# A float32r/bf16 QKV projection: another order of the products in a pair, and a padded identity tile

## The chip, the cores and the metric

The kernel runs on one core of a Trainium2 chip. The metric is device time in microseconds of one execution; the time given is the median of several runs, and one further execution was profiled.

In the profile, PE is the matrix engine, PEld its loading of the stationary operand (128 x 128, ahead of each matmul), DVE the vector engine, ACT the scalar engine, POOL the GpSimd engine. SP is used here only to issue DMAs. A matmul here has a stationary operand of 128 x 128 and a moving operand of 128 x 512 or 128 x 256; it adds its result into a PSUM bank of 128 x 512 float32. SBUF is the memory that the operands lie in; an address in the text is a byte offset within each of its 128 partitions.

## The reference

```python
def reference(x, w_qkv):            # x: 16 x 512 x 768, w_qkv: 768 x 2304, float32
    qkv = np.matmul(x, w_qkv)
    q = qkv[..., :768]
    k = qkv[..., 768:1536]
    v = qkv[..., 1536:]
    return np.stack([q, k, v], axis=0).astype(np.float32)
```

So it is one matrix product, 8192 x 768 by 768 x 2304, whose columns are split over three outputs.

## The kernel before

The 8192 rows are cut into 32 blocks of 256 rows, p = 0 to 31. The 2304 columns are cut into two groups of 1024 (q = 0 and q = 1) and 256 columns between them, the direct columns.

For p = 3 to 31 each group of 1024 columns is computed with seven products of half size in place of eight (the Winograd form of Strassen's scheme): the block of x is split into a 2 x 2 of 128 rows by 384, the weights into a 2 x 2 of 384 by 512. One block of rows with one group of columns is a `Quad`, and one pair is the two quads of one block p: a with q = 0 and b with q = 1. `do(u, n)` makes product n of quad u. Every product is three matmuls, one for each 128 of the 384 (L206):

- Products 1 and 2 are bf16: stationary xb (x rounded to bf16, by POOL, L169), moving b1.
- Products 3 to 7 are float32r: stationary s (five sums of blocks of x, made by POOL, L177 to L181), moving t1 to t4 (four sums of weight blocks) or b22 (product 3).

Below, "a6" is `do(a, 6)`, and so on. Every quad uses three PSUM banks. Bank x takes product 1, is copied by ACT into c11 (L220), then takes product 6 on top and is copied into c12 (L227), then 7 into c22 (L233), then 4 into c21 (L237): each of these products waits until ACT has read what was in the bank before. Bank z takes product 2, which DVE adds to c11 (L224). Bank y takes product 5, which DVE adds to c22 (L234), and then 3 on top, which DVE adds to c12 (L240). There are eight banks in all, given out in turn.

`rem(p)` computes the direct columns of a block in bf16: 12 matmuls of 256 columns (L256) into one bank, one copy by ACT (L266), one store by SP (L267). `store_quad` has SP store a quad (L247, L248 for a; L251, L252 for b).

A pair is written out by hand in `two` (p = 3 to 30). Its argument `early` is called behind product 1 of both quads: it has DVE transpose the next block of x (L124), POOL round it and make its sums, and SP and ACT issue the loads of the block after that (L120, two each). Before the change the order is: a1 b1, early, a2 b2, direct columns, a6 b6 a5 a7 b5 b7 a4 a3, store a, b4 b3, store b. The last block (p = 31) runs in `last`, in another order: a1 b1 a2 a6 b2 b6, a5 a7 b5 b7, a4, half of the direct columns, b4 a3 b3, the other half.

Blocks p = 0 to 2 are computed plainly in bf16 (`block`, L381) while the weights arrive and are turned into sums.

The tiles lie in SBUF in the order in which their pools are made. In the program of before the first pool has w_rem at 16512, b1 at 19584 and 25728, b22 at 31872 and 38016, t_0 (the four t of q = 0) at 44160, zero, tiny, and last eye (the identity that PE's transposes use) at 69792, 256 bytes. Behind it come the other pools: t_1 (the four t of q = 1) at 70048 and 82336, bt, o, the staging tiles, orem, xin, xf, xb from 201120 on, and s at 213408 and 221088. Every tile behind eye is a multiple of 512 bytes long. Within b1, b22, the t, xb and s the slices that one matmul takes are 1024, 2048, 2048, 256 and 512 bytes long.

Of the kernel before, what the change touches and what calls it, by code (L numbers as in the profile page):

```python
# [10 lines left out]
def kernel(  # L11
# [20 lines left out]
    nc = tc.nc  # L32
    P = 128
# [15 lines left out]
    bf16 = mybir.dt.bfloat16  # L49
# [9 lines left out]
    w_pool = ctx.enter_context(tc.tile_pool(name="w", bufs=1))  # L59
# [77 lines left out]
    def copy_halves(dst, src, two):  # L137

        nc.vector.tensor_copy(out=dst[0], in_=src[0])  # L139
        if two:  # L140
            nc.scalar.activation(dst[1], src[1], ident)  # L141
        else:
            nc.vector.tensor_copy(out=dst[1], in_=src[1])
# [3 lines left out]
    def cast_rows(p, two=True):  # L147
        src = xin.pop(p)
        xc[p] = s_pool.tile([P, 2, K], bf16, name="xc", tag="s")
        for r in range(2):  # L150
            halves = (slice(0, K // 2), slice(K // 2, K))
            copy_halves([xc[p][:, r, n] for n in halves], [src[:, r, n] for n in halves], two)

    def turn_rows(p, two=True):
        c = xc.pop(p)
        xb[p] = xb_pool.tile([P, KT, 2 * P], bf16, name="xb")
        for r in range(2):
            cols = c[:, r, :].rearrange("m (p j) -> m j p", j=KT)
            ps = ps_pool.tile([P, KT, P], bf16, name="ps")
            for j in range(KT):  # L160
                nc.tensor.transpose(ps[:, j, :], cols[:, j, :], eye[:])  # L161
            ks = (slice(0, KH), slice(KH, KT))
            copy_halves(
                [xb[p][:, n, r * P:(r + 1) * P] for n in ks], [ps[:, n, :] for n in ks], two
            )
# [29 lines left out]
    def product(u, n, ps, start):  # L195
        t1, t2, t3, t4 = ts[u.q]
        if n <= 2:
            h = (n - 1) * KH
            lhs = [xb[u.p][:, h + j, :P] for j in range(KH)]
            rhs = [b1[u.q][:, h + j, :] for j in range(KH)]  # L200
        else:
            k, t = {3: (4, b22[u.q][:]), 4: (0, t4), 5: (1, t1), 6: (2, t2), 7: (3, t3)}[n]
            lhs = [sr[u.p][:, k, j, :] for j in range(KH)]
            rhs = [t[:, j, :] for j in range(KH)]
        for j in range(KH):
            nc.tensor.matmul(  # L206
                ps[:], lhs[j], rhs[j],
                start=(start and j == 0), stop=(j == KH - 1), skip_group_check=True,
            )

    def bank():
        return ps_pool.tile([P, CB], fp32, name="ps")

    def do(u, n):
        c11, c12 = u.o[:, 0, :CB], u.o[:, 0, CB:]
        c21, c22 = u.o[:, 1, :CB], u.o[:, 1, CB:]
        if n == 1:
            u.x = bank()
            product(u, 1, u.x, True)
            nc.scalar.activation(c11, u.x[:], ident)  # L220
        elif n == 2:
            u.z = bank()
            product(u, 2, u.z, True)
            nc.vector.tensor_tensor(c11, c11, u.z[:], op=add)  # L224
        elif n == 6:
            product(u, 6, u.x, False)
            nc.scalar.activation(c12, u.x[:], ident)  # L227
        elif n == 5:
            u.y = bank()
            product(u, 5, u.y, True)  # L230
        elif n == 7:
            product(u, 7, u.x, False)
            nc.scalar.activation(c22, u.x[:], ident)  # L233
            nc.vector.tensor_tensor(c22, c22, u.y[:], op=add)  # L234
        elif n == 4:
            product(u, 4, u.x, False)
            nc.scalar.activation(c21, u.x[:], ident)  # L237
        elif n == 3:
            product(u, 3, u.y, False)
            nc.vector.tensor_tensor(c12, c12, u.y[:], op=add)  # L240

    def rows_of(s, p, lo, hi):
        return out_flat[s, p * 2 * P:(p + 1) * 2 * P, lo:hi].rearrange("(r m) n -> m r n", m=P)

    def store_quad(u):
        if u.q == 0:
            nc.sync.dma_start(rows_of(0, u.p, 0, H), u.o[:, :, :H])  # L247
            nc.sync.dma_start(rows_of(1, u.p, 0, 2 * CB - H), u.o[:, :, H:])  # L248
        else:
            part = 2 * H - Q_OFF[1]  # L250
            nc.sync.dma_start(rows_of(1, u.p, H - part, H), u.o[:, :, :part])  # L251
            nc.sync.dma_start(rows_of(2, u.p, 0, H), u.o[:, :, part:])  # L252

    def rem_row(p, r, ps):
        for j in range(KT):
            nc.tensor.matmul(  # L256
                ps, xb[p][:, j, r * P:(r + 1) * P], w_rem[:, j, :],
                start=(j == 0), stop=(j == KT - 1), skip_group_check=True,
            )

    def rem(p):
        ps = ps_pool.tile([P, 2, REM], fp32, name="ps")
        for r in range(2):
            rem_row(p, r, ps[:, r, :])
        o = or_pool.tile([P, 2, REM], fp32, name="orem")
        nc.scalar.activation(o[:], ps[:], ident)  # L266
        nc.sync.dma_start(rows_of(1, p, R_OFF - H, R_OFF - H + REM), o[:])  # L267

    def two(a, b, early):

        do(a, 1)
        do(b, 1)
        early()
        do(a, 2)
        do(b, 2)
        rem(a.p)
        do(a, 6)
        do(b, 6)
        do(a, 5)
        do(a, 7)  # L280
        do(b, 5)
        do(b, 7)
        do(a, 4)
        do(a, 3)
        store_quad(a)
        do(b, 4)
        do(b, 3)
        store_quad(b)

# [51 lines left out]
    load_rows(0)  # L341
    tiny = w_pool.tile([P, 1], fp32, name="tiny")
    nc.scalar.activation(tiny[:], zero[:, :1], ident)
    eye = w_pool.tile([P, P], bf16, name="eye")
    make_identity(nc, eye)
    load_rows(1)
    load_blocks(0, 0, 1)
# [64 lines left out]
    busy(11)  # L412
    cast_rows(0)
    turn_rows(0)
    busy(4)
    cast_rows(1)
    cast_k(0)
    cast_k(1)
    turn_rows(1)
    for j in range(2, KT):  # L420
        cast_k(j)
# [7 lines left out]
    rem(1)  # L429
    cast_rows(2, False)  # L430
    turn_rows(2, False)
    block(0, 0, b1[0], halves((4, 5)), nothing)
    for h in range(2):
# [20 lines left out]
    for p in range(NS, NP):  # L454
        def early():
            if p + 1 < NP:
                transpose(p + 1)
                round_x(p + 1)
                sums_x(p + 1)
            if p + 2 < NP:  # L460
                load_x(p + 2, nc.scalar)

        if p < NP - 1:
            two(quad(p, 0), quad(p, 1), early)
        else:
            last(quad(p, 0), quad(p, 1))
# [30 lines left out]
```

## Time and profile before

| | |
|---|---|
| median of 3 runs | 366.98 us (366.81 to 367.72) |
| the profiled execution, whole | 366.81 us |
| its span, first to last instruction | 365.0 us |
| mean granted clock of PE | 0.998 |
| data read from and written to HBM | 32.24 MB and 75.50 MB, 295 GB/s over the span |
| chain that ended last | PE 96% of the span (L206 75%, L256 11%, L381 9%) |

The span is what the profile's rows cover; the rest of the 366.81 us lies before the first and behind the last instruction. Matmuls are pipelined: the profile's end of one is modelled and lies behind the start of the next, so the time that a matmul costs is read from start to start. A few records of matmuls are missing in a trace. In the page's groups, the number after the bar is the busy time in microseconds, then the mean of one in nanoseconds, and after the second bar the idle time ahead of them. In the chain of waits a row is start, length, engine, tile and line. In the timeline it is start, length, engine, line and operation, with the idle time ahead of it and what ended that in brackets.

### The profile page before, as it was taken

Reading aid. Unit: us, or ns where it says so; the run is one execution under the profiler, and the core shown is the slowest. Engines: PE = TensorE matmul, PEld = TensorE weight load, DVE = VectorE, ACT = ScalarE, POOL = GpSimd, SP = SyncE. Lnnn points to the kernel's source line nnn. Section 1 sums busy time; section 2 is a strip of 40 time slices with the busy share of each in tenths; the row PEclk is TensorE's granted clock in tenths of the full one; section 3 lists DMA queues with packets and bytes.
Section 4 is the critical chain, followed back from the end, with each engine's and each line's share of the span. In section 5 each row is a group of like instructions: output and inputs, shape, how many; then the busy total and the mean of one; then the engine's idle time right before and its main releaser. Section 6 shows DMA issues by size and latency. Waiting matters only on the chain.

```text
span 365.0 us, 5220 instructions
## 1 busy us (share of the span) xinstructions
PE 356.6 (98%) x1765; PEld 248.2 (68%) x1797; DVE 224.5 (61%) x239; ACT 182.6 (50%) x304; POOL 173.8 (48%) x180
## 2 busy tenths in 40 slices
PE   8999999999999999999999999999999999999995
PEld 3544577676777766777676777767777777677763
DVE  3589756775565675556676556676556676556642
ACT  4557554545544444544444544444545454545452
POOL 0000961755665444665444665444666444566410
PEclk9999999999999999999999999999999999999999
DMA  7999979989999999999999999898989998999766
GB/s 300 382 372 337 342 260 334 336 294 283 284 307 302 286 281 264 301 297 311 283 286 266 299 284 321 283 281 279 293 273 317 297 291 271 291 274 326 265 248 240
DMA packets 80617, 108.08 MB, mean 296 GB/s; under 512 B 4816, under 2 KB 60368, under 8 KB 80592
## 3 DMA queue, kind: packets, MB, share of 16 engines
q1 hardware_dynamic: 65184, 96.35, 83.3%
q10 hardware_dynamic: 15408, 11.41, 9.8%
q8 instruction: 14, 0.23, 0.3%
q14 instruction: 11, 0.09, 0.1%
HBM read 32.24 MB, written 75.50 MB: 295 GB/s over the span
## 4 chain that ended last, share of the span: by engine, by line
PE 96%; ACT 1%; issue 1%; ACTq 0%; DVE 0%
PE ps L206 75%; PE ps L256 11%; PE ps L381 9%; PE ps L361 1%; PE ps L161 1%; ACT o L237 0%; ACTq L297 0%; ACT xb L141 0%; ACT orem L311 0%; DVE xb L139 0%; ACT xc L141 0%; ACTq L313 0%; DVE zero L340 0%; ACTq L311 0%
## 5 line engine op out<-in xcount | busy, mean ns | idle before, releaser
L206 PE MATMUL ps<-t,s 128*128 128x512 f32 x696 | 174.0, 398 | 0.0
L206 PEld LDWEIGHTS ps<-t,s 128*128 128x128 f32 x696 | 128.6, 188 | 28.7
L169 POOL CAST xb<-xf 128x1536 bf16<-128x1536 f32 x29 | 43.9, 1513 | 171.6 <-DVE xf L124 171.6
L234 DVE TENSOR_TENSOR o<-o,ps 128x512 f32<-128x512 f32 x58 | 39.8, 687 | 92.8 <-ACT o L233 92.8
L124 DVE STREAM_TRANSPOSE xf<-xin 128x1536 f32<-128x1536 f32 x29 | 85.5, 2949 | 6.1 <-DMA xin<-in_x_dram 3.2
L206 PE MATMUL ps<-b,xb 128*128 128x512 bf16 x320 | 74.1, 379 | 1.9
L206 PEld LDWEIGHTS <-xb 128*128 128x128 bf16 x348 | 31.7, 98 | 41.7 <-issue 7.8
L233 ACT ACTIVATE o<-ps 128x512 f32<-128x512 f32 x58 | 34.7, 598 | 46.1 <-PE ps L206 46.1
L240 DVE TENSOR_TENSOR o<-o,ps 128x512 f32<-128x512 f32 x58 | 39.9, 688 | 23.5 <-PE ps L206 21.2
L206 PE MATMUL ps<-b,s 128*128 128x512 f32 x174 | 49.7, 395 | 0.0
L237 ACT ACTIVATE o<-ps 128x512 f32<-128x512 f32 x58 | 34.7, 599 | 25.8 <-PE ps L206 22.4
L256 PE MATMUL ps<-w_rem,xb 128*128 128x256 bf16 x384 | 47.2, 273 | 0.0
L220 ACT ACTIVATE o<-ps 128x512 f32<-128x512 f32 x58 | 34.7, 598 | 24.1 <-DVE o L240 20.9
L266 ACT ACTIVATE orem<-ps 128x512 f32<-128x512 f32 x31 | 18.5, 598 | 55.7 <-PE ps L256 51.8
L256 PEld LDWEIGHTS <-xb 128*128 128x128 bf16 x384 | 37.3, 98 | 11.4 <-issue 0.5
L227 ACT ACTIVATE o<-ps 128x512 f32<-128x512 f32 x58 | 34.7, 598 | 7.0 <-PE ps L206 1.5
L206 PEld LDWEIGHTS ps<-b,s 128*128 128x128 f32 x174 | 32.6, 188 | 8.1 <-POOL xb L169 0.3
L224 DVE TENSOR_TENSOR o<-o,ps 128x512 f32<-128x512 f32 x58 | 36.3, 666 | 2.0 <-ACT o L220 1.3
L178 POOL TENSOR_TENSOR s<-s,xf 128x384 fp32r<-128x384 f32 x29 | 30.0, 1033 | 2.3
L177 POOL TENSOR_TENSOR s<-xf 128x384 fp32r<-128x384 f32 x29 | 30.9, 1067 | 0.0
L179 POOL TENSOR_TENSOR s<-xf 128x384 fp32r<-128x384 f32 x29 | 29.6, 1020 | 0.0
L181 POOL TENSOR_TENSOR s<-xf,s 128x384 fp32r<-128x384 f32 x29 | 29.3, 1010 | 0.0
(36 smaller groups left out, 128.1 us busy)
## 6 DMA issues: line engine op xcount, KB each, us to landing
out_dram<-o SPq DMA_DIRECT2D x62, 768.0 KB, 5.4
out_dram<-o SPq DMA_DIRECT2D x65, 256.0 KB, 4.6
xin<-in_x_dram SPq DMA_DIRECT2D x62, 192.0 KB, 6.9
xin<-in_x_dram ACTq DMA_DIRECT2D x54, 192.0 KB, 4.2
out_dram<-orem SPq DMA_DIRECT2D x31, 256.0 KB, 5.5
st<-in_w_qkv_dram SPq DMA_DIRECT2D x6, 768.0 KB, 14.1
xin<-in_x_dram SPq DMA_DIRECT2D x3, 768.0 KB, 5.7
st<-in_w_qkv_dram SPq DMA_DIRECT2D x6, 256.0 KB, 6.1
```

The source lines that it names most:

```text
L124: nc.vector.transpose(t[:].rearrange("p j (g b) -> p g j b", b=G), xin.pop(p)[:].rearrange("p g (a j) -> p g j a", a=G),)
L169: nc.gpsimd.tensor_copy(out=xb[p][:], in_=xf[p][:])
L206: nc.tensor.matmul(ps[:], lhs[j], rhs[j], start=(start and j == 0), stop=(j == KH - 1), skip_group_check=True,)
L220: nc.scalar.activation(c11, u.x[:], ident)
L224: nc.vector.tensor_tensor(c11, c11, u.z[:], op=add)
L227: nc.scalar.activation(c12, u.x[:], ident)
L233: nc.scalar.activation(c22, u.x[:], ident)
L234: nc.vector.tensor_tensor(c22, c22, u.y[:], op=add)
L237: nc.scalar.activation(c21, u.x[:], ident)
L240: nc.vector.tensor_tensor(c12, c12, u.y[:], op=add)
L256: nc.tensor.matmul(ps, xb[p][:, j, r * P:(r + 1) * P], w_rem[:, j, :], start=(j == 0), stop=(j == KT - 1), skip_group_check=True,)
L381: nc.tensor.matmul(ps[n][:], xb[p][:, j, r * P:(r + 1) * P], w[:, j, :], start=(j == 0), stop=(j == KT - 1), skip_group_check=True,)
```

## The change

It has two parts. In `two` the order becomes a1 b1, early, a2 a6 b2 b6 a5 a7 b5 b7 a4, direct columns, b4 a3, store a, b3, store b. And eye is made 240 bf16 columns wide instead of 128, of which the first 128 are used, so that it takes 480 bytes instead of 256, and every tile behind it lies 224 bytes further on: t_1, xb and s then lie as far past a multiple of 512 bytes as w_rem, b1, b22 and t_0. `last` and the blocks p = 0 to 2 keep their order.

```diff
-                nc.tensor.transpose(ps[:, j, :], cols[:, j, :], eye[:])
+                nc.tensor.transpose(ps[:, j, :], cols[:, j, :], eye)
...
         do(b, 1)
         early()
         do(a, 2)
+        do(a, 6)
         do(b, 2)
-        rem(a.p)
-        do(a, 6)
         do(b, 6)
         do(a, 5)
         do(a, 7)
         do(b, 5)
         do(b, 7)
         do(a, 4)
+        rem(a.p)
+        do(b, 4)
         do(a, 3)
         store_quad(a)
-        do(b, 4)
         do(b, 3)
         store_quad(b)
...
-    eye = w_pool.tile([P, P], bf16, name="eye")
+
+    eye = w_pool.tile([P, 240], bf16, name="eye")[:, :P]
     make_identity(nc, eye)
```

## Prediction

> **What bounds the kernel now.** I read the page first, then the chain of waits in order of time, then the timeline of one steady pair and of the last pair, and at the end the starts of single matmuls.
>
> ```profile
> span 365.0 us, 5220 instructions
> PE 356.6 (98%) x1765; PEld 248.2 (68%) x1797; DVE 224.5 (61%) x239; ACT 182.6 (50%) x304; POOL 173.8 (48%) x180
> PEclk9999999999999999999999999999999999999999
> DMA  7999979989999999999999999898989998999766
> GB/s 300 382 372 337 342 260 334 336 294 283 284 307 302 286 281 264 301 297 311 283 286 266 299 284 321 283 281 279 293 273 317 297 291 271 291 274 326 265 248 240
> L206 PE MATMUL ps<-t,s 128*128 128x512 f32 x696 | 174.0, 398 | 0.0
> L206 PE MATMUL ps<-b,xb 128*128 128x512 bf16 x320 | 74.1, 379 | 1.9
> ```
>
> PE is busy for 98% at the full clock, and in front of the float32r products it never idles. The chain says the same for each pair:
>
> ```profile
> 212.03 6.97 PE ps L206 x30
> 219.00 0.07 issue
> 219.06 2.54 PE ps L206 x11
> 221.60 1.31 PE ps L256 x12
> 222.91 6.97 PE ps L206 x30
> ```
>
> A pair takes 222.91 - 212.03 = 10.88 us (10.887 from the single starts), all PE. There is no wait to take away. The time changes only if the PE stream itself gets shorter or if a new wait appears.
>
> Start to start, bf16 matmuls of 512 columns stand 216 ns apart and the direct ones of 256 columns 109 ns. Twelve of each make 2.59 + 1.31 = 3.90 us, so the 30 float32r matmuls with their boundaries take 6.99 us. Inside their run they stand 232.4 ns apart, 16.6 ns more than bf16 at the same width. That surplus is where the padding could act.
>
> **Part 1, the padding.** In the program of before, w_rem, b1, b22 and t_0 lie 128 bytes past a multiple of 512; everything behind eye (t_1, xb, s) lies 416 past. Padded, eye takes 480 bytes and all lie at 128. So before has both cases side by side: stationary s always at 416; moving tile at another offset for a6, a5, a7, a4, a3 (t_0, b22) and b3 (b22); at the same offset for b6, b5, b7, b4 (t_1). The mean durations of the six matmuls of a5 and a7, then of b5 and b7, in a steady pair, then the same two sixes in the last pair:
>
> ```profile
> L206 PE MATMUL ps<-t,s 128*128 128x512 f32 x6 | 1.6, 396 | 0.0
> ...
> L206 PE MATMUL ps<-t,s 128*128 128x512 f32 x6 | 1.5, 393 | 0.0
> ...
> L206 PE MATMUL ps<-t,s 128*128 128x512 f32 x6 | 1.6, 394 | 0.0
> ...
> L206 PE MATMUL ps<-t,s 128*128 128x512 f32 x6 | 1.5, 390 | 0.0
> ```
>
> The second of each two, at one offset, is shorter by 3 to 4 ns. These ends are modelled, so I took starts, over 25 steady pairs (p = 6 on). Different offsets: 233.6 ns (16 places). Same offset: 230.8 (12 places; b6 233.3, 230.8, 226.7; b5 230.0, 235.8, 228.4; b7 232.5, 230.8, 226.7; b4 230.0, 235.8, 228.4). In p = 3 and p = 5 the classes stand at 232.7 and 228.7, in the last pair at 232.6 and 229.5. b3, in unit b but with its tile in the other pool, goes with the first class (233.3): offset, not unit, sorts them. The lowest value, 226.7 ns, comes five times running in b5 and b7 of p = 3 and of the last pair, never in unit a there.
>
> With one offset I put all 30 at 229.6, the mean of 230.8, 228.7 and 229.5: (232.4 - 229.6) x 30 = 84 ns a pair. Bounds: all at 226.7 gives 171 ns; all at the worst same-offset value, 235.8, costs 102 ns; no effect is 0.
>
> [...] The rows above differ by offset, and I go with the rows.
>
> The padding costs no instruction: the identity is written and read at the same width, for 36 transposes of 2.7 us in all. bf16 matmuls exist at both relations too (bt with xb at one, b1 with xb at two) and run at 216 ns in both: 0. xin, xf, o and orem shift as well; their engines and queues have slack, below.
>
> **Part 2, the order.** Same instructions. Now each pair changes type six times instead of twice. The last pair of before already runs a1 b1 a2 a6 b2 b6 ... a4, direct, b4 a3 b3:
>
> ```profile
> 349.70 1.89 PE L206 MATMUL ps<-b,xb 128*128 128x512 bf16 x8
> 351.24 1.05 PE L206 MATMUL ps<-t,s 128*128 128x512 f32 x3
> 352.13 0.82 PE L206 MATMUL ps<-b,xb 128*128 128x512 bf16 x3
> 352.60 4.50 PE L206 MATMUL ps<-t,s 128*128 128x512 f32 x18
> 356.94 0.83 PE L256 MATMUL ps<-w_rem,xb 128*128 128x256 bf16 x6
> 357.52 0.95 PE L206 MATMUL ps<-t,s 128*128 128x512 f32 x3
> ```
>
> Into float32r, by single starts: 351.214 to 351.663 holds one bf16 and one float32r matmul, 449 = 216 + 233, nothing lost; 445 at b6; after the direct columns 342 = 109 + 233. Back to bf16: the first bf16 slot is 227 instead of 216, the first direct one 120 instead of 109: 11 each. Before, the entry after the direct columns costs 350 - 342 = 8. So per pair: two more exits, +22; one entry of 8 exchanged for three of 0, -3 and 0, -11; net +11 ns. Bounds: +38 if all three entries cost 8; -5 from the whole last pair, which takes 360.37 - 349.49 = 10.88 us in the new order (first start put one slot ahead of its first row, since a record is missing), but without POOL and transposes.
>
> **New waits.** a6 now follows a2 directly and writes the bank that ACT reads for c11:
>
> ```profile
> 208.15 0.69 DVE L240 TENSOR_TENSOR o<-o,ps 128x512 f32<-128x512 f32 x1 [0.70 <-PE ps L206]
> 208.18 2.54 PE L206 MATMUL ps<-b,xb 128*128 128x512 bf16 x11
> 208.75 2.94 DVE L124 STREAM_TRANSPOSE xf<-xin 128x1536 f32<-128x1536 f32 x1
> 208.86 1.24 ACT L220 ACTIVATE o<-ps 128x512 f32<-128x512 f32 x2 [0.81 <-DVE o L240]
> 209.53 1.23 ACTq L120 DMA_DIRECT2D xin<-in_x_dram  x2
> ```
>
> The pair begins at 207.96; a6 would start nine slots later at 209.90, a's ACTIVATE ends at 209.48: 0.42 us to spare. Behind ACT's two loads (to 210.76) waits only c12 of a6, ready at about 210.8. s[2] for the next pair is done by about 204.4 and needed at 209.9. a6's c12 is read 2 us before a7 writes. Banks are now taken in the order x, x, z, z, y, y, direct; each is reused eight later, the tightest being a2's bank, freed by c21 of b4, four products earlier. On ACT the direct copy falls between the two c21. On SP the direct store comes before both quad stores as before, later by some 5 us. Store a is ready 0.7 us later, so stores of b and the loads after them slip by about 0.4 us; the transpose that reads these loads has DVE idle time of 2.6 us behind it before the next c22 add. Were that gone, a late add would hold a3's bank. All taken as 0. DMA at nine tenths is not the limit either: 296 GB/s on average, while one slice has 382; a pair under 1% shorter asks for under 1% more.
>
> **Sum.** Per pair -84 + 11 = -73 ns; 28 pairs of this order (p = 3 to 30): -2.04 us; the last pair gains some 0.05 (16 places from 232.6 to 229.5). The profiled execution took 366.81 (span 365.0, 1.8 around it): 364.7. The median of the runs is 0.17 above it: 364.9.
>
> **Rivals.** (1) One offset lets the chain of matmuls settle at 226.7, as it does in five in a row: -171 + 11 = -160 ns, x 28 = -4.5 us, 362.5. For: runs at one offset get 9 and 15 long instead of 3 and 6. Against: b5 and b7 do not settle in the steady pairs. (2) The padding does not do what it says: the classes differ by place in the pair. Then only the order counts: +0.3 us (-0.1 to +1.1), 367.3. For: places within a class scatter by 9 ns, more than the classes differ; against: b3. (3) Slower: at one offset both streams start in the same phase, and the bad places of the same class, the second of b5 and b4 at 235.8, become the rule: +102 + 11 = 113 ns, +3.2 us, 370.1. It decides from a mean above 232.0; above 233.3 the loss passes 0.3%. Against: eight of twelve same-offset places lie below 232.0.
>
> **How the numbers follow.** Forecast, means of 228 to 231.0: 363.6 to 366.1, 0.5. Rival 1: 0.15. Rival 2, with gains too small to see: 0.2. Rival 3: 0.15. Runs of this kernel tell no change from 0.3%, 1.1 us. The forecast's upper end and part of rival 2 lie within that: faster 0.61, same 0.24, slower 0.15. The range runs from rival 1's value, 362.5, up to rival 2's, 367.3, and leaves out rival 3 and little at the bottom.
>
> **What would show it.** Right: pairs of 10.81 us in the chain; t,s and b,s matmuls with shorter means (396 to about 392) in both units alike; no PE idle in front of a6, and 11 ns lost behind a6, a4 and b3 each. Wrong: float32r starts still 232 or more apart, a difference left between units a and b, or idle time before L206 released by ACT L220.

## The result and the profile after

The changed kernel takes 365.01 us in the median of 6 runs (364.97 to 365.77), before 366.98 (366.81 to 367.72): a ratio of 0.9945, 95% interval 0.9932 to 0.9958. So it is faster by 0.55%; the prediction said 364.9 us. The profiled execution took 364.97 us, with a span of 362.8.

The page of the changed kernel, the same groups as before:

```profile
span 362.8 us, 5242 instructions
PE 354.3 (98%) x1765; PEld 244.0 (67%) x1797; DVE 224.2 (62%) x239; ACT 182.2 (50%) x304; POOL 173.8 (48%) x180
PEclk9999999999999999999999999999999999999998
DMA  7999969988899888999888899888899889899767
L206 PE MATMUL ps<-t,s 128*128 128x512 f32 x696 | 186.5, 410 | 0.0
L206 PE MATMUL ps<-b,xb 128*128 128x512 bf16 x320 | 79.0, 380 | 1.9
L206 PE MATMUL ps<-b,s 128*128 128x512 f32 x174 | 44.5, 391 | 0.0
```

PE is still the bound at 98%, with a granted clock of 0.997. One row misleads, and the prediction had named it as a sign of being right: the mean of the t,s matmuls rose from 398 to 410 ns although they run closer together. Its ends are modelled: records of 388 to 397 ns start 226 to 239 ns apart in the pair below. The first matmul of a float32r run is booked with 480 to 580 ns, and there are now three such runs per pair instead of one. The b,s matmuls, which never begin a run, fell from 395 to 391.

The chain of waits of the changed kernel, over one steady pair and the beginning of the next:

```profile
207.01 7.34 PE ps L206 x32
214.34 1.33 PE ps L256 x12
215.67 2.07 PE ps L206 x9
217.74 0.07 issue
217.81 7.34 PE ps L206 x32
```

A pair takes 217.81 - 207.01 = 10.80 us, 10.807 by the starts of single matmuls (10.81 was forecast), against 10.887 before. Over 28 pairs that is 2.24 us. The last pair gains 0.07, the start and the end lose 0.12, and the sum is the 2.2 us between the spans. The execution as a whole fell by less, 1.84 us (366.81 to 364.97), because more time lies outside the span: 2.2 us instead of 1.8. This goes with the order: it is 2.1 to 2.2 us in every run of the three kernels with the new order (changed, e2 and e10 below) and 1.7 to 1.8 in every other run. What it is spent on, the runs do not show.

Start to start, by place in the pair, in ns (means over the steady pairs, rounded; the first interval of each float32r run is left out, since the record of its first matmul is misplaced: in both traces it starts 28 ns behind the bf16 matmul before it):

```
before  run of 30:  234 233 233 231 227 234 235 232 235 232 235 230 236 228 232 231 227 234 235 232 235 232 235 230 236 228 232 234
after   run of 3:   229
        run of 18:  232 231 227 227 227 227 227 227 227 227 227 227 227 227 227 227
        run of 9:   231 236 228 232 231 227 227
```

The long run settles at 226.7 ns and stays there, in unit a as in unit b.

### The profile page after: what moved, and what is told of

It is laid out like the page before. It is cut to its first block, busy times and chain, and to the rows that moved or that the text cites. A ratio compares the mean times of both kernels' runs of the same rounds, so it can differ in the third digit from the quotient of the medians.

```text
span 362.8 us, 5242 instructions
## 1 busy us (share of the span) xinstructions
PE 354.3 (98%) x1765; PEld 244.0 (67%) x1797; DVE 224.2 (62%) x239; ACT 182.2 (50%) x304; POOL 173.8 (48%) x180
## 4 chain that ended last, share of the span: by engine, by line
PE 96%; ACT 1%; issue 1%; ACTq 0%; DVE 0%
PE ps L206 75%; PE ps L256 11%; PE ps L382 9%; PE ps L362 1%; PE ps L161 0%; ACT o L237 0%; ACTq L297 0%; ACT xb L141 0%; ACT orem L311 0%; DVE xb L139 0%; ACT xc L141 0%; ACTq L313 0%; DVE zero L340 0%; ACTq L311 0%
## 5 line engine op out<-in xcount | busy, mean ns | idle before, releaser
L206 PE MATMUL ps<-t,s 128*128 128x512 f32 x696 | 186.5, 410 | 0.0
L169 POOL CAST xb<-xf 128x1536 bf16<-128x1536 f32 x29 | 46.4, 1600 | 169.5 <-DVE xf L124 167.5
L124 DVE STREAM_TRANSPOSE xf<-xin 128x1536 f32<-128x1536 f32 x29 | 87.2, 3008 | 9.1 <-DMA xin<-in_x_dram 6.5
L206 PE MATMUL ps<-b,xb 128*128 128x512 bf16 x320 | 79.0, 380 | 1.9
L206 PEld LDWEIGHTS <-xb 128*128 128x128 bf16 x348 | 29.4, 98 | 42.7 <-issue 15.3
L206 PE MATMUL ps<-b,s 128*128 128x512 f32 x174 | 44.5, 391 | 0.0
L256 PEld LDWEIGHTS <-xb 128*128 128x128 bf16 x384 | 35.1, 98 | 12.0 <-issue 7.8
L177 POOL TENSOR_TENSOR s<-xf 128x384 fp32r<-128x384 f32 x29 | 29.3, 1010 | 0.0
L179 POOL TENSOR_TENSOR s<-xf 128x384 fp32r<-128x384 f32 x29 | 29.1, 1002 | 0.0
```

The lines of the kernel that those rows point to most:

```text
L124: nc.vector.transpose(t[:].rearrange("p j (g b) -> p g j b", b=G), xin.pop(p)[:].rearrange("p g (a j) -> p g j a", a=G),)
L169: nc.gpsimd.tensor_copy(out=xb[p][:], in_=xf[p][:])
L206: nc.tensor.matmul(ps[:], lhs[j], rhs[j], start=(start and j == 0), stop=(j == KH - 1), skip_group_check=True,)
L256: nc.tensor.matmul(ps, xb[p][:, j, r * P:(r + 1) * P], w_rem[:, j, :], start=(j == 0), stop=(j == KT - 1), skip_group_check=True,)
```

## The experiments

In all of them the whole computation is done. The offset of a tile is meant modulo 512 bytes. "Pair" is the period of the steady pairs, from starts of single matmuls; it repeats within 1 ns, or in a fixed pattern where more than one number is given. A ratio compares with runs of before that were made beside those of the kernel; "one run" means that there is a single time, while its pair is still read from some 25 pairs.

| | order | s past the moving tiles | pair, us | median, us | ratio to before, 95% |
|---|---|---|---|---|---|
| before | old | 288 (t_0, b22), 0 (t_1) | 10.887 | 366.98 | |
| changed | new | 0 | 10.807 | 365.01 | 0.9932 to 0.9958 |
| e1_pad_only | old | 0 | 10.760 | 363.26 | 0.9881 to 0.9911 |
| e2_order_only | new | 288, 0 | 10.873 | 366.90 | 0.9988 to 1.0006 |
| e3_s256 | old | 256 | 10.760 | 363.43 | 0.9889 to 0.9916 |
| e4_all416 | old | 0 | 10.760 | 364.01 | 0.9903 to 0.9930 |
| e5_s32 | old | 32 | 10.907 | 367.52 | 1.0003 to 1.0022 |
| e6_s64 | old | 64 | 10.920 | 368.13 | one run |
| e7_s16 | old | 16, 80 in turn | 10.729, 10.877 | 365.12 | one run |
| e8_s48 | old | 48, 112 in turn | 10.906, 10.921 | 368.38 | one run |
| e9_s16_both | old | 16 | 10.908, 10.916, 10.729 | 366.06 | 0.9961 to 0.9981 |
| e10_s16_order | new | 16 | 10.936, 10.817 | 367.25 | 0.9995 to 1.0014 |
| e11_s8_both | old | 8 | 10.843 | 366.26 | one run |
| e12_s128 | old | 128 | 10.890 to 10.912 | 367.23 | one run |

**One part at a time.** e1 takes the padding and leaves the order:

```diff
-    eye = w_pool.tile([P, P], bf16, name="eye")
+    eye = w_pool.tile([P, 240], bf16, name="eye")[:, :P]
```

> Padded identity, order of before: all 30 float32r products of a pair in one run at one offset. If the offset sets the spacing and a run settles at 226.7 ns start to start after some five matmuls, as the run of 15 does in the changed kernel, a pair takes about 12 x 216 + 12 x 109 + 30 x 226.7 + 25 (settling) + 22 (one entry, one exit) = 10.75 us against 10.81 changed and 10.89 before, and the kernel 363.4 us. If the gain of the change came from its order, or the padding pays only together with it, 365 us or more, up to 367.

Measured 363.26 us. The chain of e1:

```profile
210.19 6.84 PE ps L206 x30
217.04 0.07 issue
217.10 2.54 PE ps L206 x11
219.64 1.31 PE ps L256 x12
220.95 6.84 PE ps L206 x30
```

Where before has 6.97 for the 30 float32r matmuls, this has 6.84; the other rows of the pair are the same, and PE waits for nothing in either. By starts, averaged as above, the run settles from the tenth interval listed on:

```
e1      run of 30:  229 234 236 224 231 236 228 232 231 227 227 226 227 226 226 227 226 226 227 226 226 227 226 226 227 226 226 227
```

e2 takes the order and leaves eye at 256 bytes:

```diff
         do(a, 2)
+        do(a, 6)
         do(b, 2)
-        rem(a.p)
-        do(a, 6)
...
         do(a, 4)
+        rem(a.p)
+        do(b, 4)
         do(a, 3)
         store_quad(a)
-        do(b, 4)
```

> New order of the pair, identity tile of 256 bytes as before. By the prediction's sum the order costs 11 ns a pair (-5 to +38): 367.3 us (366.9 to 368.1), with float32r starts still apart by unit (a near 233.6, b near 230). If the order brought the gain: 365.

Measured 366.90 us, not told apart from before. The chain of e2:

```profile
208.05 7.39 PE ps L206 x32
215.44 1.33 PE ps L256 x12
216.77 2.09 PE ps L206 x9
218.86 0.07 issue
218.93 7.39 PE ps L206 x32
```

A pair is 10.88 (10.873 by starts), 14 ns shorter than before; over 28 pairs that is 0.39 us, and the 0.36 us more outside the span take it back. So, within the pairs, the padding alone is worth 127 ns a pair under the old order and 66 under the new one; the order alone gains 14 without the padding and loses 47 with it. The two parts are not additive, and all of the gain in the kernel's time is the padding's. Of the 1.75 us between e1 and the changed kernel, 28 x 47 ns are 1.3 and the time outside the span 0.36.

**What about the offset counts.** e3 keeps the padding and moves s alone:

```diff
+    sp_pool = ctx.enter_context(tc.tile_pool(name="sp", bufs=1))
     s_pool = ctx.enter_context(tc.tile_pool(name="s", bufs=2))
...
+    sp_pool.tile([P, 128], bf16, name="sp")
```

> Padded identity, order of before, and s alone moved on by 256 bytes: s at 384 past a multiple of 512, every moving tile at 128. If the relation of the two operands modulo 512 counts, the float32r starts go back to 232 to 236 ns and the time to 366.5 to 369. If it counts modulo 256, or if s only has to lie at a multiple of 64 or 128 bytes, it is as with the padding alone, near 363.4.

The pair is 10.760 us as in e1, start for start. So the tiles need not lie at one offset modulo 512: 256 between s and the moving tiles is as good as 0.

e4 moves all of them together, to the address at which the tiles behind eye lay before:

```diff
+    w_pool.tile([P, 144], bf16, name="wpad")
     w_rem = w_pool.tile([P, KT, REM], bf16, name="w_rem")
```

> Order of before, padded identity, and 288 bytes more ahead of the first pool: w_rem, b1, b22, t_0, t_1, xb and s all at 416 past a multiple of 512, so at one offset but none at a multiple of 64. If only the relation counts: as with the padding alone, near 363.4. If the address itself has to be at a multiple of 64 or 128: near 367.

The steady pairs are again 10.760 us: the relation counts, not the address itself. The kernel is 0.75 us slower than e1 all the same. In its trace one early pair takes 11.098 us, where the weight loads wait for POOL. The waits of e4 in that pair:

```profile
DVE xf L125 <- DMA xin<-in_x_dram: 1.9, 1, 1.9
...
PEld ps L207 <- POOL xb L170: 0.5, 1, 0.5
```

A transpose waits for its load of x, and xb comes late. That is 0.34 us that occurs once and is no matter of the spacing. The rest of the 0.75 lies ahead of the first pair: its float32r work starts at 48.93 us instead of 48.56. What delays that, the runs do not show.

e5 and e6 move s as e3 does, by 32 and by 64 bytes.

> Padded identity, order of before, s alone moved on by 32 bytes. Before, s and t_0 differed by 288 bytes, which is 32 modulo 64, 128 and 256, and 256 alone made no difference. If the 32 left over is what costs, all 30 starts of a pair go to the 233.6 ns of unit a before: 10.92 us a pair, 368 us. If the whole 288 was needed, near 363.3.

> The same with 64 bytes. If the relation counts modulo 64, the spacing is 226.7 ns in the settled run and a pair 10.76 us, 363.3 us. If it counts modulo 128 or 256: starts of 232 or more, 367 us or more.

Both lose the gain and more. The starts of e5 alternate between 235 and 232 and never settle lower, those of e6 stay at 233 to 234. The chain of e5, in which bf16 and float32r matmuls of 512 columns are merged (30 + 12):

```profile
213.03 9.60 PE ps L208 x42
222.63 1.31 PE ps L258 x12
223.94 9.60 PE ps L208 x42
```

A pair takes 10.91 us in e5 and 10.92 in e6. So a relation modulo 64 is excluded: 64 is bad where 0 and 256 are good. e5's mean, 233.1, is near unit a's 233.6 of before, whose 288 bytes are 256 + 32: with e3 it is the 32 that cost, not the 256. e12 moves s by 128:

> Padded identity, order of before, s moved on by 128 bytes in both buffers. 256 was as good as 0, and 32 and 64 were bad. If the relation repeats every 128 bytes: 10.76 us a pair, 363.3 us. If it repeats only every 256: starts of 232 to 234 ns, 10.91 us, 367.5 us.

Starts from 225 to 241 ns, 10.890 to 10.912 us a pair. With that a relation modulo 128 is excluded too; 256 fits all that was tried, though only the distances 0 and 256 speak for it.

**Is there a better distance than 0?** e7 and e8 move s within its tile (the tile is 64 bytes longer, so that the second buffer lies another 64 further on):

```diff
-        s = s_pool.tile([P, 5, KH, P], f32r, name="s")
+        s = s_pool.tile([P, 5 * KH * P + 16], f32r, name="s")[:, 4:4 + 5 * KH * P]
+        s = s.rearrange("p (k j m) -> p k j m", k=5, j=KH)
```

> s moved on by 16 bytes within its tile (both buffers of s equal modulo 64). If only equal offsets modulo 32 or 64 settle at 226.7, starts go up towards 232 to 236, 367 to 369 us; if the cost grows with the distance, half of what 32 bytes cost; if 16 is a better phase than 0, settled starts below 226.7 and less than 363 us.

> s moved on by 48 bytes within its tile. If the relation counts modulo 64 and by distance, as with 16 bytes the other way round; if modulo 32, exactly as with 16 bytes.

They were written with a period of 64 in mind, which e6, beside them, excluded. Read modulo 256, e8 has s at 48 and 112 in turn, and both are bad (10.906 and 10.921). In e7 the steady pairs with s at 16 took 10.729 us, less than any other, their intervals at 227 from the third on; those with s at 80 took 10.877. From that came a theory: 16 bytes make a run settle at once. e9 puts both buffers there, in two pools of their own (16 bytes into the first, 240 into the second, which begins 32 bytes further on modulo 256); e11 does the same with 8, and e10 is e9 under the new order.

```diff
-    s_pool = ctx.enter_context(tc.tile_pool(name="s", bufs=2))
+    s_pools = [ctx.enter_context(tc.tile_pool(name=f"s{n}", bufs=1)) for n in range(2)]
...
-        s = s_pool.tile([P, 5, KH, P], f32r, name="s")
+        n, w = (4, 60)[p % 2], 5 * KH * P
+        s = s_pools[p % 2].tile([P, n + w], f32r, name="s", tag="s")[:, n:n + w]
+        s = s.rearrange("p (k j m) -> p k j m", k=5, j=KH)
```

> Padded identity, order of before, and both buffers of s 16 bytes past the offset of the moving tiles modulo 256 (with s moved on by 16 in one buffer and by 80 in the other, pairs alternated between 10.729 and 10.877 us; here both stand at 16). If it is the 16 that gave the short pairs: all pairs 10.73 us, 28 x 31 ns below the padding alone, 362.4 us. If it was the 80, or the alternation itself: 10.80 or more and 364 us or more.

The theory fell: 366.06 us. The chain of e9, three pairs in a row:

```profile
212.10 9.60 PE ps L208 x42
221.69 1.31 PE ps L258 x12
223.00 9.61 PE ps L208 x42
232.61 1.31 PE ps L258 x12
233.92 9.42 PE ps L208 x42
243.34 1.31 PE ps L258 x12
```

Two pairs stand at 9.60 and 9.61 for their 42 matmuls of 512 columns, the third at 9.42. With the same distance a run of 30 keeps either 231 to 236 ns throughout, or 227 from its third interval on. The pattern comes every third pair, so it does not go with the two buffers of s. That it goes with the state in which a run is entered is a guess: x is loaded into three buffers in turn (xin), and no run changes their number. Against xin speaks e10, which has the same three and repeats every second pair. In e7 too the place did not decide alone: its pairs at 16 each followed a pair at 80 and were short from p = 8 on, but that of p = 6 stood at 233.3 ns.

> The same places of s under the changed kernel's order. The starts of the changed kernel, summed against a settled 226.7 ns, put 52 ns a pair on the three ways back from float32r to bf16 and 53 on entries and settling, against 14 and 45 with the order of before. If that is right, s at 16 leaves the ways back: about 38 ns above the pairs of the order of before, near 10.77 us, 363.5 us. If the order costs nothing once runs settle at once: 362.4; if short runs never settle: 365 as the changed kernel.

Pairs of 10.936 and 10.817 us in turn, counted from one run of 18 to the next (10.922 and 10.831 from one group of direct columns to the next): the run of 18 stands at 233.2 and at 226.7 ns in turn, the same two-sidedness under the new order, so it could not say what the order costs once runs settle at once.

> s at 8 bytes instead of 16, both buffers. If any small lead of s over the moving tile settles at once: 10.73 us a pair, 362.4 us; if the steps are of 16 bytes: as with 0, 10.76 us and 363.3; worse than both if an offset within 16 bytes costs by itself.

Starts go round in fives, 234 230 231 229 229, and never settle: 10.843 us. So none of the distances tried beats 0 or 256 reliably, and e1 is the fastest version found: 0.89% to 1.19% below before by its interval, 1.75 us below the changed kernel.

## Why the prediction was right

**The bound.** PE, with no wait to remove, and a gain that had to come from the stream itself: right, in the kernel after and in e1.

**The padding.** Right: the two classes that stood side by side in the trace before (233.6 and 230.8 ns) differ by offset, and making all alike made unit a as fast as unit b (both at 226.7 ns where the run has settled). e5 closes the case against the rival that the classes differ by their place in the pair: the same order and places, s moved by 32 bytes, 147 ns a pair lost against e1. The granted clock was 0.997 in e1 and 0.999 in e5, PE waited for nothing in the steady pairs, and the spacing of the matmuls changed with the place of the stationary tile alone, from a mean of 228.1 ns to 233.1. What in the chip makes that place count, the runs do not show.

**The size of it.** I put all 30 at 229.6 ns, 84 ns a pair. Under the old order the padding gave 127, with a mean of 228.1; rival 1's settling at 226.7 is what really happens, but only after a run has gone through some unsettled matmuls, two of the intervals listed in the changed kernel's run of 18, nine in e1's run of 30. It was held against rival 1 that b5 and b7 did not settle in the steady pairs; six at one offset were too few to show it.

**The order.** I put it at +11 ns. Without the padding it measured -14, 9 ns below the bounds of -5 to +38; with the padding +47, 9 ns above them. The term was sized from the last pair before, whose float32r matmuls stood mostly at 229 to 235, whichever way they were entered, and settled in one stretch only. Here, where the long run settles, cutting it cost more. The starts of the changed kernel, each taken above 226.7, 216 or 109, put 52 ns on the three ways back to bf16 (24 behind a6, 14 behind a4 and b3 each) and 53 on entries and settling; e1 has 14 and 45. So the loss lies mostly in two further ways back, 38 of 47 ns, where 11 each had been read: behind a6 the last float32r slot is 239 ns instead of 226.7, while in the last pair before it was 233, no longer than the others. The entries, put at -11 against before, came to +8. This split is read from the starts of the two kernels; no run tests it by itself.

**The sum.** -84 + 11 = -73 was forecast, -127 + 47 = -80 measured. Both terms were undersized, the gain by 43 ns and the cost by 36. (Counted with the order first it is -14 and -66, and both terms miss the other way; only their sum does not depend on which is counted first.) The total was right to 7 ns a pair, 0.2 us, because the two errors cancel, which is luck. A third term was off as well: the sum kept 1.8 us outside the span, and it was 2.2. That took back more than the 0.2 us that the pairs had gained beyond the forecast, so that 364.9 stands beside 365.01.

**No new wait.** Right. The timeline of the changed kernel where a6 follows a2:

```profile
207.58 3.00 DVE L124 STREAM_TRANSPOSE xf<-xin 128x1536 f32<-128x1536 f32 x1
207.69 1.25 ACT L220 ACTIVATE o<-ps 128x512 f32<-128x512 f32 x2 [1.49 <-DVE o L240]
208.35 1.62 ACTq L120 DMA_DIRECT2D xin<-in_x_dram  x2
208.54 1.04 PE L206 MATMUL ps<-t,s 128*128 128x512 f32 x3
210.02 0.60 ACT L227 ACTIVATE o<-ps 128x512 f32<-128x512 f32 x1 [1.09 <-PE ps L206]
```

a's c11 is copied by 208.29, as the single records have it; a6's first matmul comes behind the bf16 matmul of 208.517, at 208.73: 0.44 us to spare, where 0.42 was reckoned. ACT's loads end at 209.97, just ahead of c12 at 210.02. DMA is busy nine tenths of these pairs and moves 292 GB/s.

**Rival 3,** that one offset would be the bad state, was wrong for 0: e1 shows 235 or 236 only in the first intervals of a run. It describes e5 and e6, at other distances.

## What to carry to other kernels

Where PE is the bound and float32r matmuls stand further apart than bf16 ones of the same width (before 232.4 ns against 216), compare start to start by the place of the operands, before looking for waits: here 32 bytes between the offsets of stationary and moving tile cost 147 ns in a pair of 10.8 us (e5 against e1). Where the runs settle, keep the float32r products in one long run: cutting it cost 47 ns a pair here. Two edits that touch the same stream should be measured apart: here the better kernel is one of them alone.

## What was not expected

Equal addresses do not make equal times: with s 16 bytes past the moving tiles, a run of 30 stays at 233.4 ns or at 226.9 for all its length, in a fixed pattern of three pairs, 10.908, 10.916 and 10.729 us. In before, in the changed kernel and in e1 to e6 the steady pairs repeat within 1 ns. And the distance does not work by its size: 256 bytes apart is as good as 0, while 8 bytes already cost 83 ns a pair.
